# A sixth slot in the ring of norm statistics: every activation tile of a two-layer decoder trunk moves 128 bytes up

## The chip, the cores and the metric

One core of one Trainium2 chip runs the whole program. The metric is device time in microseconds (us). Three runs of the kernel before took 859.58, 862.08 and 862.19 us, so the median is 862.08 us. Lower is better.

## What is computed

The reference is a decoder trunk of two layers on 256 tokens of width 1024, in float32. In each layer:

- h = RMSNorm(x). One projection of h gives the inputs of three token mixers and three gates. The mixers are sliding-window attention, a diagonal state-space recurrence (S5) with a gated linear unit, and a causal convolution of 31 taps with a layer norm.
- The three results, each times the sigmoid of its gate, are added, projected, and added to x.
- A SwiGLU feed-forward of hidden width 2816 follows: x + (silu(RMSNorm(x) Wg) * (RMSNorm(x) Wu)) Wo.
- A gated per-layer embedding is added: x + sigmoid(RMSNorm(x) Wp) * (p We).

A last RMSNorm gives the output. There are thus seven norms: three in each layer and the last one.

## The kernel before

**Tiles and stages.** The 256 tokens are two tiles (t = 0, 1) of 128 partitions. Every product with a weight is done by `gemm` (lines 468 to 488): the weights stream through SBUF in blocks of 128 x 1024 floats (512 KB), each split into a rounded part `wh` (ScalarE, a cast, line 176) and its remainder `wl` (VectorE, a subtraction, line 200). The activations are split the same way into `hi` and `lo` tiles. Each product is three TensorE matmuls of 512 columns, hi*wh, hi*wl and lo*wh, in which the activation slice of 128 x 128 is the loaded (stationary) operand and the weight slice of 128 x 512 is the streamed (moving) one. They are all recorded at line 227, so the rows tell them apart by their tiles: `zk`, `zq`, `zc` and `g` (input projection and gates), `ya`, `yg`, `yc` (mixer outputs), `mo` (mixer projection), `fz` and `fo` (feed-forward in and out), `ez`, `pz` and `pl` (embedding and its gate). `yx` is the S5 output, made of many float32 matmuls of 64 columns. TensorE also does the transposes (line 307: `hT`, `sT` and others).

**Order.** The program is written out in one fixed order for each engine by a planner in the file itself, which books estimated costs per tile and lets small streams of vector and scalar work in between the matmuls. The planner looks at names of tiles and of ring slots that it has given itself (`keys`, line 102), for the weights and the PSUM banks; it does not look at addresses, and the tiles of norm statistics are not among those that it aliases. All DMAs are issued by SP's queue.

**Pools and addresses.** SBUF tiles come from three pools that are laid one after the other in each partition: `cp` (constants, x, the S5 tables), `wp` (the weight rings `raw`, `wh`, `wl`) and `act` (all activation tiles). Inside `act` each tag is a ring of slots, and the rings lie in the order in which their tags are first used. The first call in the schedule is

```python
        def norm_stats():
            return act.tile([128, 16, NT], F32, tag="nst", bufs=5, name="nst")
```

so the ring `nst` is the first of the pool. One tile of it is 16 x 2 floats, 128 bytes per partition. It is asked for seven times, once for each norm: for the first input norm (in the main body), and in each call of `layer` for the feed-forward norm (`fst`), the embedding gate's norm (`pst`) and the next input norm or the last norm (`nst`). With five slots the sixth request (`pst` of the second layer) takes the slot of the first one, and the seventh (the last norm) takes that of the second.

Who touches such a tile: `norm_half` (line 496) sums squares into it on ScalarE (tile `sqj` holds the squares), `norm_end` (line 501) makes 1/sqrt(mean) in it on GpSimd (POOL), and the scalings of `zk`, `zq`, `zc`, `g`, `fz` and `pz` read it.

The byte addresses in each partition, as the built program has them (ring starts; the last column is the address modulo 256, which is the same for all slots of a ring whose slot size is a multiple of 256):

| tiles | pool | start | modulo 256 |
|---|---|---|---|
| x0, x1 | cp | 18112, 22208 | 192 |
| ones, sdT, brow (bias rows and their factors) | cp | 28544, 29056, 30080 | 128 |
| ubuf (convolution input; 1144 bytes per channel half) | cp | 34176 | 128 |
| CAr (S5 table; the matmul for index j reads from byte 640*j + 128 of it) | cp | 44896 | 96 |
| raw, wh, wl | wp | 67424, 79712, 96096 | 96 |
| nst (5 slots) | act | 112480 | 96, then 224 and 96 in turn |
| 4096-byte tiles: feature tiles h, m, f, p (hi and lo), M, e, fgb | act | 113120 | 224 |
| 1024-byte tiles: fth, sqj, cacc, gtm, tb and others | act | 149984 | 224 |
| zqk, vt, kT | act | 161760 | 224 |
| 2048-byte tiles: hd, gt, sT, aT, cT, qT, v, sw and others | act | 168928 | 224 |
| Sr, Si (last) | act | 224672, ends at 228896 | 160 |

Of the kernel before, what the change touches and what calls it, by code (L numbers as in the profile page):

```python
# [6 lines left out]
F32 = mybir.dt.float32  # L7
# [9 lines left out]
NT = 2  # L17
# [64 lines left out]
def trunk_kernel(tc, wts, par, bmat, cst_d, x_d, pos_d, pt_d, bias_d, fg_d, out_d, dbg=None):  # L82
# [3 lines left out]
    with ctx:  # L86
        cp = ctx.enter_context(tc.tile_pool(name="cp", bufs=1))
        wp = ctx.enter_context(tc.tile_pool(name="wp", bufs=5))
        act = ctx.enter_context(tc.tile_pool(name="act", bufs=2))
# [398 lines left out]
                    pump(slack)  # L488

        def norm_stats():  # L490
            return act.tile([128, 16, NT], F32, tag="nst", bufs=5, name="nst")

        def stat(sts, i, t):
            return sts[:, i, t:t + 1]
# [601 lines left out]
        def layer(l, feat, sts, prep):  # L1096
# [156 lines left out]
            mT.upto(2)  # L1253

            fst = norm_stats()
            fT = []

# [52 lines left out]
            def hid_lhs(t, k):  # L1310
                while len(hid) <= k // 2:
                    push()
                return hid[k // 2][0][:, t, k % 2, :], hid[k // 2][1][:, t, k % 2, :]

            pst = norm_stats()
            gT = []
            for n in range(2):
# [16 lines left out]
            gT[0].upto(2)  # L1334

            nst = norm_stats()
            nT = []

# [311 lines left out]
```

## Time and profile before

| | |
|---|---|
| median of three runs | 862.08 us |
| the profiled execution's own time | 860.29 us |
| its span, first to last instruction | 858.5 us |
| mean granted TensorE clock in it | 0.994 of full speed |
| TensorE (PE) busy | 840.4 us, 98% |
| weight loads of TensorE (PEld) busy | 686.8 us, 80% |
| VectorE (DVE) busy | 580.9 us, 68% |
| ScalarE (ACT) busy | 457.2 us, 53% |
| GpSimd (POOL) busy | 126.8 us, 15% |

How to read the profile: times are us from the span's start unless marked ns. A line "L200 DVE TENSOR_TENSOR wl<-raw,wh" is the group of instructions of line 200 on VectorE that write `wl` from `raw` and `wh`. A matmul's own duration (394 ns) is longer than the step from one to the next (233 ns), since matmuls are pipelined; time is lost or won only in the steps. "idle before" is time in which the engine did nothing, with what it waited for.

### The profile page before, as it was taken

How to read it: one execution, taken by the hardware profiler on the slowest of the kernel's cores; microseconds unless marked ns; L12 is line 12 of the kernel's file. 1: busy time of each engine (PE TensorE's matmuls, PEld its weight loads, DVE VectorE, ACT ScalarE, POOL GpSimd, SP SyncE). 2: the span in 40 equal slices, each digit the busy share in tenths (PEclk: the TensorE clock that was granted, in tenths of full speed). 3: DMA queues.
4: the chain of work that ended last, by engine and by line, in shares of the span. 5: the costliest groups of instructions: out<-in, count | busy, mean ns of one | idle time of the engine just before them, and what ended most of it. 6: DMA issues, size and time to landing. Idle time of an engine off the chain costs nothing.

```text
span 858.5 us, 11139 instructions
## 1 busy us (share of the span) xinstructions
PE 840.4 (98%) x3976; PEld 686.8 (80%) x3976; DVE 580.9 (68%) x865; ACT 457.2 (53%) x745; POOL 126.8 (15%) x325
## 2 busy tenths in 40 slices
PE   8989999899999999999999999999999999999996
PEld 7877788688888888888888878878888888888885
DVE  4688875887667784654577599568766666654555
ACT  5675756345556666543564554544554454444454
POOL 5787001000744200000020000100000000000001
PEclk9999999989999999999999999999999999999999
DMA  7554533436765654666654443655566666666661
GB/s 252 181 178 138 152 120 98 123 99 180 211 173 177 187 177 148 179 182 190 184 152 145 124 123 101 191 174 173 172 185 180 182 177 187 181 179 189 182 185 75
DMA packets 41199, 141.34 MB, mean 165 GB/s; under 512 B 4756, under 2 KB 6404, under 8 KB 41144
## 3 DMA queue, kind: packets, MB, share of 16 engines
q1 hardware_dynamic: 41144, 140.64, 55.2%
q8 instruction: 31, 0.51, 0.2%
q14 instruction: 24, 0.20, 0.1%
HBM read 139.49 MB, written 1.13 MB: 164 GB/s over the span
## 4 chain that ended last, share of the span: by engine, by line
PE 88%; ACT 4%; DVE 3%; DMA 2%; POOL 1%; issue 1%; SPq 0%; POOLq 0%; ACTq 0%; DVEq 0%
PE fz L227 29%; PE g L227 15%; PE fo L227 14%; PE mo L227 5%; PE pz L227 4%; PE yg L227 3%; DMA raw<-in_wts 2%; PE ya L227 2%; PE sc L227 2%; PE pl L227 1%; PE zq L227 1%; PE ez L227 1%; PE zc L227 1%; PE yc L227 1%; PE yx L227 1%; ACT wh L176 1%
## 5 line engine op out<-in xcount | busy, mean ns | idle before, releaser
L200 DVE TENSOR_TENSOR wl<-raw,wh 128x1024 fp32r<-128x1024 f32 (+1 forms) x261 | 316.2, 1215 | 212.5 <-ACT wh L176 212.4
L176 ACT CAST wh<-raw 128x1024 fp32r<-128x1024 f32 (+1 forms) x261 | 271.6, 1043 | 205.2 <-PE fo L227 57.0
L200 POOL TENSOR_TENSOR nst<-nst 128x2 f32<-128x2 f32 (+1 forms) x14 | 2.8, 199 | 538.9 <-ACT sqj L171 538.4
L227 PE MATMUL fz<-wh,f0h 128*128 128x512 f32 x176 | 70.9, 403 | 0.0
L227 PE MATMUL fz<-wh,f1h 128*128 128x512 f32 x176 | 70.4, 400 | 0.0
L227 PE MATMUL fo<-wh,hdh 128*128 128x512 f32 x176 | 69.8, 397 | 0.0
L227 PE MATMUL fz<-wh,f1l 128*128 128x512 f32 x176 | 69.6, 395 | 0.0
L227 PE MATMUL fz<-wh,f0l 128*128 128x512 f32 x176 | 69.5, 395 | 0.0
L227 PE MATMUL fo<-wh,hdl 128*128 128x512 f32 x176 | 69.5, 395 | 0.0
L227 PE MATMUL fo<-wl,hdh 128*128 128x512 f32 x176 | 69.5, 395 | 0.0
L227 PE MATMUL fz<-wl,f1h 128*128 128x512 f32 x176 | 69.5, 395 | 0.0
L227 PE MATMUL fz<-wl,f0h 128*128 128x512 f32 x176 | 69.4, 394 | 0.0
L227 PEld LDWEIGHTS fo<-wh,hdl 128*128 128x128 f32 x176 | 33.1, 188 | 7.9
L227 PEld LDWEIGHTS fz<-wh,f1l 128*128 128x128 f32 x176 | 33.1, 188 | 7.9
L227 PEld LDWEIGHTS fz<-wh,f0l 128*128 128x128 f32 x176 | 33.1, 188 | 7.8
L227 PEld LDWEIGHTS fo<-wh,hdh 128*128 128x128 f32 x176 | 33.1, 188 | 7.7
L227 PE MATMUL g<-wh,h1h 128*128 128x512 f32 x96 | 38.7, 403 | 0.6 <-DVE M L210 0.6
L227 PEld LDWEIGHTS fo<-wl,hdh 128*128 128x128 f32 x176 | 33.1, 188 | 7.6
L227 PEld LDWEIGHTS fz<-wl,f1h 128*128 128x128 f32 x176 | 33.1, 188 | 7.5
L227 PEld LDWEIGHTS fz<-wh,f1h 128*128 128x128 f32 x176 | 33.1, 188 | 7.4
L227 PE MATMUL g<-wh,h0h 128*128 128x512 f32 x96 | 39.0, 406 | 0.0
L227 PEld LDWEIGHTS fz<-wl,f0h 128*128 128x128 f32 x176 | 33.2, 188 | 7.2
(390 smaller groups left out, 1766.6 us busy)
## 6 DMA issues: line engine op xcount, KB each, us to landing
raw<-in_wts SPq DMA_DIRECT2D x258, 512.0 KB
raw<-in_wts SPq DMA_DIRECT2D x4, 256.0 KB
out<-e SPq DMA_DIRECT2D x4, 256.0 KB
x<-in_x SPq DMA_DIRECT2D x4, 128.0 KB
x<-in_x SPq DMA_DIRECT2D x2, 256.0 KB
bm<-in_bmat SPq DMA_DIRECT2D x4, 128.0 KB
pT<-in_pt SPq DMA_DIRECT2D x2, 256.0 KB
fgb<-in_fg SPq DMA_DIRECT2D x1, 512.0 KB
```

The source lines that it names most:

```text
L176: ACT.copy(out=out, in_=in_)
L200: (eng or DVE).tensor_tensor(out=out, in0=a, in1=b, op=op)
L227: PE.matmul(out, lhsT, rhs, start=start, stop=stop)
```

## The change

The ring gets a sixth slot:

```diff
         def norm_stats():
-            return act.tile([128, 16, NT], F32, tag="nst", bufs=5, name="nst")
+            return act.tile([128, 16, NT], F32, tag="nst", bufs=6, name="nst")
```

All that lies behind this ring in the pool `act` starts 128 bytes higher; the pools `cp` and `wp` and the ring's first five slots stay where they are. The sixth request for statistics takes a slot of its own, and the seventh takes the slot of the first request. No computing instruction, no transfer and no place in any engine's order is added or taken away by the edited line.

## Rows read from the trace of the kernel before

**Rows 1.** The page's first part: span, and busy time of each engine.

```profile
span 858.5 us, 11139 instructions
PE 840.4 (98%) x3976; PEld 686.8 (80%) x3976; DVE 580.9 (68%) x865; ACT 457.2 (53%) x745; POOL 126.8 (15%) x325
```

**Rows 2.** The page's fourth part: the chain that ended last, by engine.

```profile
PE 88%; ACT 4%; DVE 3%; DMA 2%; POOL 1%; issue 1%; SPq 0%; POOLq 0%; ACTq 0%; DVEq 0%
```

**Rows 3.** The chain of waits in order of time: start, length, what.

```profile
265.31 11.20 PE fz L227 x48
...
382.37 29.27 PE fo L227 x126
...
762.76 29.39 PE fo L227 x126
```

**Rows 4.** Windows of the span: busy (count) by engine, granted clock, DMA share, GB/s.

```profile
core 0: us, PE busy (x) PEld busy (x) DVE busy (x) ACT busy (x) POOL busy (x), PEclk, DMA share, GB/s
165.00:169.80 4.80, 1.83 (x10) 1.21 (x9) 3.28 (x6) 1.95 (x3) 0.00 (x0) 1.00 0.71 219
169.80:176.70 6.90, 5.94 (x16) 4.43 (x16) 3.41 (x7) 1.92 (x3) 0.00 (x0) 0.51 0.24 63
855.80:858.50 2.70, 0.00 (x0) 0.00 (x0) 0.00 (x0) 0.00 (x0) 0.00 (x0) 0.52 0.46 173
```

**Rows 5.** Groups by shape, TensorE, operands moved (hi tiles) and unmoved (brow, sdT).

```profile
L227 PE MATMUL fo<-wl,hdh 128*128 128x512 f32 x176 | 69.5, 395 | 0.0
L227 PE MATMUL fz<-wl,f1h 128*128 128x512 f32 x176 | 69.5, 395 | 0.0
L227 PE MATMUL g<-wl,h1h 128*128 128x512 f32 x96 | 37.9, 394 | 0.0
L227 PE MATMUL g<-brow,sdT 128*128 128x512 f32 x24 | 9.5, 394 | 0.0
```

**Rows 6.** Instructions of tile yx: duration min/median/max in ns, first and last start.

```profile
L227 PEld LDWEIGHTS yx<-Sr,CAr x32: 192/192/193, 160.0 to 476.1; 128*128 128x128 f32 x32
L227 PE MATMUL yx<-Sr,CAr x32: 275/275/276, 160.1 to 476.1; 128*128 128x64 f32 x32
```

**Rows 7.** Instructions of tiles cacc, M, fth and hdh in the same form.

```profile
L210 DVE SCALAR_TENSOR_TENSOR cacc<-ubuf,cst,cacc x58: 433/479/482, 41.7 to 116.4; 128x256 f32<-128x256 f32 x58
...
L200 DVE TENSOR_TENSOR M<-M,gt x8: 691/692/693, 161.2 to 606.0; 128x512 f32<-128x512 f32 x8
L210 DVE SCALAR_TENSOR_TENSOR M<-gt,ya x8: 680/682/689, 133.5 to 579.3; 128x512 f32<-128x512 f32 x8
...
L200 DVE TENSOR_TENSOR M<-scr,cst x2: 683/684/685, 82.5 to 291.3; 128x512 f32<-128x512 f32 x2
...
L171 ACT ACTIVATE fth<-fz,nst x44: 463/475/476, 225.9 to 759.5; 128x256 f32<-128x256 f32 x44
...
L176 ACT CAST hdh<-hT x22: 585/587/588, 230.5 to 762.8; 128x512 fp32r<-128x512 f32 x22
```

**Rows 8.** Instructions of the second feed-forward's end on ScalarE, in order of time.

```profile
790.92 0.63 ACT L171 ACTIVATE sqj<-x 128x512 bf16<-128x512 f32 x1 [1.89 <-DVE x L200]
```

**Rows 9.** The chain of waits around the S5 output of the first layer.

```profile
165.37 1.47 PE ya L227 x6
166.85 0.02 issue
166.87 0.69 DVE M L210
167.56 0.61 DVE ge L200
168.17 0.02 issue
168.19 0.64 ACT ge L171
168.83 0.02 issue
168.85 0.70 DVE gy L210
169.55 0.02 issue
169.58 0.46 DVE gtm L214
170.03 0.04 issue
170.08 1.13 PE sT L307 x4
171.21 0.02 issue
171.23 0.61 ACT sTh L171
171.83 0.04 issue
171.88 8.94 PE yg L227 x28
```

**Rows 10.** TensorE in order of time after that wait.

```profile
171.88 0.79 PE L227 MATMUL yg<-wh,sTh 128*128 128x512 f32 x1 [0.69 <-ACT sTh L171]
...
175.88 0.63 PE L227 MATMUL yg<-wh,sTl 128*128 128x512 f32 x1
176.31 0.55 PE L227 MATMUL yg<-wh,sTh 128*128 128x512 f32 x1
176.70 0.39 PE L227 MATMUL yg<-wl,sTh 128*128 128x512 f32 x1
```

## The prediction

> **What bounds the kernel now.** I read the page's busy times first: TensorE is busy 840.4 of 858.5 us, VectorE 580.9 and ScalarE 457.2 [rows 1]. Then the chain that ended last: 88% of it is TensorE, and all other engines and transfers together are 12% [rows 2]. Then the chain in order of time, to see what TensorE does there: long unbroken runs of 512-column matmuls. In the feed-forward 48 of them take 11.20 us and 126 take 29.27 to 29.39 us, which is 233 ns from one to the next in both [rows 3]. So the time is, nearly everywhere, the number of matmuls times one step. What is not that step is short: the largest hole is 166.85 to 171.88 in the first layer, where the S5 output goes through VectorE and ScalarE before TensorE can take it up [rows 9], and a tail after the last matmul. An edit counts here if it changes the number of matmuls, the length of their step, one of these few holes, or the clock.
>
> The number doesn't change: the edited line adds and takes away no instruction. What is left is where the operands lie and which slot two of the statistics tiles get.
>
> **The slot.** Before, the sixth request for statistics must wait until the first tile has been read for the last time; its first writer is the square-sum that starts at 790.92, and what that instruction in fact waited for is VectorE's update of x [rows 8]. The old tile's readers are the scalings of the first layer's input projection and gates, and in the program's order all of these stand ahead of that layer's `yg` matmuls, which start at 171.88 [rows 9]. The seventh request behaves the same way with the second tile, whose readers end with the first layer's feed-forward, ahead of the `fo` run that starts at 382.37 [rows 3]. With six slots the sixth request waits for nothing and the seventh for the first tile. All these waits are satisfied hundreds of us before they are asked for, so removing or replacing them is worth 0. If a stand-alone wait instruction comes or goes with them, its price is not shown as a row of its own; the nearest rows are the gaps called "issue" in the chain, 0.02 to 0.04 us [rows 9]. Bounds: -0.08 to +0.08 us for two. I take 0.
>
> **The addresses, TensorE.** The moved operands are the stationary slices (`h`, `f`, `hd` and so on) of most 512-column matmuls; the weights stay. Before, the moved tiles lie at 224 modulo 256, after it at 96. No row shows the same tile in both places, so the cost must be bounded by operands that already lie differently. First, the bias matmul `g<-brow,sdT`: both of its operands are in the pool that stays, at 128 modulo 256, and its duration is 394 ns, against 394 and 395 ns for `g<-wl,h1h`, `fz<-wl,f1h` and `fo<-wl,hdh`, whose stationary operand is at 224 and whose moving one is at 96 [rows 5]. Second, and closest to the edit, the S5 output: the matmul for index j reads its table `CAr` from byte 640*j + 128, and 640 is two and a half times 256, so each next j stands exactly 128 bytes further modulo 256. Over 32 such matmuls the loads take 192 to 193 ns and the matmuls 275 to 276 ns [rows 6]. If a shift by 128 bytes mattered to TensorE, these would fall into two groups. So I take 0 per matmul. The bound is one step of the rows' own difference, 1 ns in 395: 0.25%. The three families whose rows stand there have 6 x 176 (`fz`), 3 x 176 (`fo`) and 6 x 96 (`g`) matmuls, 2160 in all, and 2160 x 233 ns = 503 us; 0.25% of that is 1.3 us either way.
>
> **The addresses, VectorE and ScalarE.** The convolution reads `ubuf` from a start that moves by 4 bytes with each of the 29 taps of its long row and by 1144 bytes between the two channel halves, so modulo 256 its 58 instructions sample starts from 132 up to 364, in steps of 4 bytes. Their median is 479 ns and their longest 482, so half of them lie within 3 ns wherever they start [rows 7]. VectorE's 512-element operations run in 680 to 693 ns whether their inputs are both moved tiles (`M<-M,gt`), PSUM and a moved tile (`M<-gt,ya`) or unmoved constants (`M<-scr,cst`) [rows 7]. ScalarE's forms that write moved tiles are as tight over all slots of their rings: 585 to 588 ns and 463 to 476 ns [rows 7]. I take 0. As a bound I use the whole spread of VectorE's rows, 680 against 693, 2%. It would count only where these engines are on the chain: in the hole of [rows 9] they hold 0.69 + 0.61 + 0.64 + 0.70 + 0.46 + 0.61 = 3.71 us, and 2% of it is 0.07 us; all of their share of the chain, 7% of 858.5 or 60 us [rows 2], would give 1.2 us at the very most. Elsewhere the cover is TensorE's own work: VectorE has 32% of the span free [rows 1]. If that cover were gone, a matmul group would start late by what VectorE lost, some 14 ns per operation.
>
> **The addresses, transfers.** The weight stream writes tiles that don't move. Of the moved tiles the one with a transfer at the end is the output, stored from `e`. After the last matmul the queues are busy for 0.46 of 2.70 us, or 1.2 us [rows 4]. I take 0 for it. [...]
>
> **The sum** is 0. Its bounds add up to 1.3 (TensorE) + 1.2 (VectorE and ScalarE) + 0.1 (waits) = 2.6 us either way. The profiled execution took 860.29 us; the shown runs took 859.58, 862.08 and 862.19, so it stands inside their spread of 2.6 us, and the median is near its upper end. With nothing changed I expect the mean of these four, 861.0 us, rather than the median.
>
> **The rivals.** (a) *TensorE's two reads meet.* After the change the stationary tiles stand at 96 modulo 256, as the weights do, while before they stood 128 bytes apart. If reads at the same place in such a stretch got in each other's way, each of the long runs of matmuls would slow down. As a price I take the 2% of VectorE's forms: 2% of the 503 us is 10 us, giving 871 us; it decides the sign from a step longer by 1.2 ns on (2160 x 1.2 ns = 2.6 us). Against it: `brow` and `sdT` already lie at the same place modulo 256, and their matmul takes the usual 394 ns [rows 5]. (b) *The mirror image*: the present place is the bad one and the step of 233 ns has slack that the move frees; 2% would give 851 us. The same row speaks against it. (c) *The clock.* [...] Between 171.88 and 176.70 the `yg` matmuls make eleven steps of 0.43 or 0.44 us instead of 0.233 [rows 10]: 4.82 us against 2.57, a loss of 2.25 us. [...] Without the fall: 860.29 - 2.25 = 858.0 us; with one more: 862.5, or 864.4 in a run like the highest. That two thirds of the runs lie 2.5 us above the third would fit such a difference. (d) *The tiles don't move*, because something else in the pool takes the 128 bytes up: the time would be that of the forecast.
>
> **How the numbers follow.** Two medians of this kernel less than 0.3%, 2.6 us, apart can't be told from no change. The forecast (and (d), which gives the same time) gets 0.78, since three independent rows have operands 128 bytes or less apart without any second group. (b) gets 0.06, and a median without the clock's fall 0.06: faster 0.12. (a) gets 0.06, and a median raised by a second fall 0.04: slower 0.10. The low end of the range is (c) without its fall, 858.0; the high end is the forecast with the sum's upper bound, 861.0 + 2.6 = 863.6, which lies above all shown runs. It leaves out (a), (b), the second fall in a high run and a little of the forecast, about 0.2 in all.
>
> **What would show it.** If right: `fz` still 11.20 us for 48 and `fo` 29.3 for 126; `yx`, `M`, `hdh` and `fth` within 3 ns of [rows 6, 7]; the hole at 167 of 5.0 us, with or without the low clock. Wrong on TensorE: the step off 233 ns by over 1 ns, in the families with moved stationary operands and not in `g<-brow,sdT`. Wrong on the clock: the same steps but another number of low-clock stretches. Wrong on the slot: a new wait on the statistics tiles near 790 or 835 us.

## The result, and the profile after

The changed kernel takes 847.11 us in the median of four runs (846.29 to 849.21), the kernel before 862.13 us in four (859.58 to 862.33). The ratio is 0.9836 with a 95% interval of 0.9811 to 0.9862: about 14 us or 1.6% faster (by the two medians 15 us). The forecast was no change, 858.0 to 863.6 us; rival (b) had the sign, at a chance of 0.06. The profiled execution took 846.92 us, with a span of 845.1 us against 858.5.

The first part of the page, to read beside [rows 1]:

```profile
span 845.1 us, 11139 instructions
PE 825.9 (98%) x3976; PEld 684.2 (81%) x3976; DVE 581.0 (69%) x865; ACT 458.3 (54%) x745; POOL 130.0 (15%) x325
```

The same 11139 instructions ran, in the same order on each engine. VectorE and ScalarE are busy for as long as before, to 0.1 and 1.1 us, GpSimd for 3.2 us longer. TensorE lost 14.5 us of busy time over the same 3976 matmuls. Where, the chain of waits in order of time tells, to read beside [rows 3] (start, length, what):

```profile
262.95 10.91 PE fz L227 x48
...
348.15 28.59 PE fo L227 x126
377.62 28.59 PE fo L227 x126
...
751.31 28.61 PE fo L227 x126
```

126 matmuls of `fo` take 28.59 us instead of 29.27 to 29.39: one step is 28.59 / 126 = 226.9 ns, where it was 232.3 to 233.3. Every long run is shorter: 48 of `fz` take 10.91 or 10.94 us (227.3 or 227.9 ns each) instead of mostly 11.20. Groups by shape, to read beside [rows 5]:

```profile
L227 PE MATMUL fz<-wl,f1h 128*128 128x512 f32 x176 | 68.5, 389 | 0.0
L227 PE MATMUL fo<-wl,hdh 128*128 128x512 f32 x176 | 68.5, 389 | 0.0
L227 PE MATMUL g<-wl,h1h 128*128 128x512 f32 x96 | 37.4, 390 | 0.0
...
L227 PE MATMUL g<-brow,sdT 128*128 128x512 f32 x24 | 9.4, 393 | 0.0
```

The three families with moved operands fell from 394 or 395 ns to 389 or 390. The bias matmul, whose two operands did not move, is at 393 where it was 394: what was taken for proof that place doesn't matter is now the odd one out.

The gain grows with the number of matmuls done. The second `fo` run of the first layer starts at 377.62 instead of 382.37, 4.75 us earlier, and the first of the second layer (751.31 instead of 762.76) 11.45 us earlier. Over all 512-column matmuls that follow one another within 260 ns the step fell from 232.7 to 227.8 ns in the mean. The program has 3096 such products of weights and activations, so that is worth 3096 x 4.9 ns = 15.2 us; the span is 13.4 us shorter. The first part of the gain is lost again early on: where `yx` begins (160.19 us instead of 160.07), nothing is gained yet. Windows of the span (columns as in [rows 4]), of the kernel after:

```profile
36.00:70.00 34.00, 31.00 (x142) 25.05 (x141) 29.57 (x60) 20.81 (x33) 29.54 (x72) 0.95 0.58 181
...
169.80:176.70 6.90, 5.83 (x19) 4.45 (x20) 3.76 (x7) 1.92 (x3) 0.00 (x0) 0.75 0.28 75
```

and of the kernel before:

```profile
36.00:70.00 34.00, 31.67 (x149) 25.37 (x148) 29.02 (x59) 21.78 (x33) 29.47 (x71) 1.00 0.58 177
```

From 36 to 70 us TensorE did 7 matmuls fewer, at a mean granted clock of 0.95 where it was 1.00: a new stretch of low clock, 0.50 from 65.81 to 69.21 us. The stretch after the S5 output is shorter than before instead: 0.50 from 171.62 to 175.03 us where it was 0.50 from 169.82 to 176.63, so that over the window from 169.80 to 176.70 the mean clock is 0.75 where [rows 4] show 0.51. By an estimate from these clocks the first costs 0.05 x 34 = 1.7 us and the second gives 0.24 x 6.9 = 1.7 us back, so the two cancel and are not the gain.

The instructions of VectorE and ScalarE did not change, as in [rows 7]:

```profile
L200 DVE TENSOR_TENSOR M<-M,gt x8: 691/692/692, 161.5 to 598.1; 128x512 f32<-128x512 f32 x8
...
L171 ACT ACTIVATE fth<-fz,nst x44: 463/476/477, 224.4 to 748.2; 128x256 f32<-128x256 f32 x44
```

### The profile page after: what moved, and what is told of

Same layout as the page of the kernel before. It is cut to its first block, busy times and chain, and to the rows that moved or that the text cites. A ratio compares the mean times of both kernels' runs of the same rounds, so it can differ in the third digit from the quotient of the medians.

```text
span 845.1 us, 11139 instructions
## 1 busy us (share of the span) xinstructions
PE 825.9 (98%) x3976; PEld 684.2 (81%) x3976; DVE 581.0 (69%) x865; ACT 458.3 (54%) x745; POOL 130.0 (15%) x325
## 4 chain that ended last, share of the span: by engine, by line
PE 88%; POOL 4%; ACT 3%; issue 1%; DVE 1%; DMA 1%; SPq 1%; POOLq 0%; ACTq 0%; DVEq 0%
PE fz L227 28%; PE g L227 15%; PE fo L227 14%; PE mo L227 5%; PE pz L227 4%; PE yg L227 3%; PE sc L227 2%; PE ya L227 2%; POOL scr L205 2%; PE pl L227 1%; PE zq L227 1%; PE ez L227 1%; PE yc L227 1%; POOL scr L200 1%; PE yx L227 1%
```

## The experiments

Four theories were set against each other. S: the sixth slot frees a wait. P: the place of the loaded (stationary) operand sets TensorE's step. R: what counts is how the loaded operand lies to the streamed one. W: the writes of other engines into the moved tiles disturb TensorE. All kernels give the step of a matmul, read from long runs in the chain of waits as length by count. One run has one time and one profile unless an interval is given.

**The move without the slot, and the slot without the move.**

```diff
+            act.tile([128, 32], F32, tag="pad", bufs=1, name="pad")
             sts = norm_stats()
```

> The ring keeps its five slots; an unused tile of 128 bytes stands in front of it, so the activation tiles lie where the changed kernel has them and the statistics tiles take turns as in the kernel before. Theory P (the place of the loaded operand sets TensorE's step) and its rivals R (the distance between loaded and streamed operand) and W (VectorE's and ScalarE's writes into the moved tiles disturb TensorE's reads): step of the 512-column matmuls 226.7 ns, 48 of fz in 10.9 us, time 847 us within 2. Theory S (the sixth slot frees a wait): step 233.3 ns, 11.20 us, 862 us.

847.83 us in the median of four, ratio 0.9861 (0.9831 to 0.9890). The other way round:

```diff
-            return act.tile([128, 16, NT], F32, tag="nst", bufs=5, name="nst")
+            return act.tile([128, 12, NT], F32, tag="nst", bufs=6, name="nst")
...
+            act.tile([128, 16], F32, tag="pad", bufs=1, name="pad")
             sts = norm_stats()
```

> Six slots of 96 bytes and an unused tile of 64 bytes: 640 bytes as in the kernel before, so no activation tile moves, but the sixth request has a slot of its own. P, R and W: step 233.3 ns, time 862 us within 2. S: 226.7 ns, 847 us.

859.46 us beside 860.11, the median of the kernel before in that session. The chain of the first kernel:

```profile
348.14 28.59 PE fo L227 x126
```

and of the second:

```profile
351.52 29.39 PE fo L227 x126
```

S falls: the slot does nothing that these runs can tell, the 128 bytes do all of it.

**Part of the tiles moves.**

```diff
+            if l == 0:
+                act.tile([128, 32], F32, tag="pad", bufs=1, name="pad")
             S["Ux"] = Ux = b2([128, 8, 64], name="Ux")
```

> An unused tile of 128 bytes ahead of the ring of 2048-byte tiles alone: hd, sT, aT, cT, pT and gt move, the feature tiles h, m, f and p stay. P and R: fo, ya, yg, yc and ez step at 226.7 ns, while fz, g, mo, pz and the input projection stay at 233.3; about 1000 matmuls x 6.6 ns = 6.6 us less, 855 us within 2. W: no split by the loaded operand; fz steps change as much as fo steps, since both run beside the same writes. S: nothing changes, 862 us.

```profile
739.57 11.20 PE fz L227 x48
...
762.79 28.61 PE fo L227 x126
```

`fo`, whose loaded tiles moved, steps at 227 ns; `fz`, beside the same writes in the same run, at 233. W falls, and the gain goes with the operand that a matmul loads. The time, 858.76 us beside 860.11, is less of a gain than forecast. The families that moved hold 816 such products by the program, not about 1000, worth 4 us at 4.9 ns each. Also, this run has a low-clock stretch early on which the profile before lacks (a mean clock of 0.95 from 36 to 70 us, and 0.991 over the run), and `yx` begins at 162.28, 2.2 us behind it.

**Another distance.**

```diff
+            act.tile([128, 8], F32, tag="pad", bufs=1, name="pad")
             sts = norm_stats()
```

> An unused tile of 32 bytes in front: the loaded slices of 512 bytes start on a multiple of 512 instead of 480 (before) or 96 (after) modulo 512. P: if what costs is how a slice lies across a boundary of 512 or 256 bytes, this place has the least of it, step at most 226.7 ns, time at most 847 us. R (a distance of 128 bytes to the weights modulo 256 is bad, none is good; here it is 160 modulo 256): nearer to the kernel before, 230 to 233 ns, 855 to 862 us. S: 862 us.

862.88 us; the chain:

```profile
353.76 29.41 PE fo L227 x126
```

That is 233.4 ns: slices that start exactly on a multiple of 512 bytes are no better. P in its natural form, a slice crossing a boundary, is refuted here.

**Weights and activations move together, and the weights alone.** Both have the first line; the second kernel has one statistics slot fewer, so that the activation tiles stand where they stood.

```diff
         M4 = cp.tile([128, 8, 64], F32, name="M4")
+        cp.tile([128, 32], F32, name="pad")
...
-            return act.tile([128, 16, NT], F32, tag="nst", bufs=5, name="nst")
+            return act.tile([128, 16, NT], F32, tag="nst", bufs=4, name="nst")
```

> An unused tile of 128 bytes at the end of the constants' pool, ahead of the weight rings: weights and activation tiles both move by 128 bytes, so the loaded slices stand where the changed kernel has them and their distance to the weights is that of the kernel before. Theory P (place of the loaded operand alone): step 226.7 ns, fz 10.9 us for 48, time 847 us within 2. Rival R (distance of loaded and streamed operand): step 233 ns, 862 us.

> The same unused tile ahead of the weight rings, and one slot fewer (four) in the ring of statistics: the weights move by 128 bytes, the activation tiles stand where the kernel before has them. P: step 233 ns, 862 us. R: the distance is that of neither kernel; the weights now stand at the same place modulo 512 as the loaded slices, so a change either way from 233 ns, by over 3 ns, 853 us or 870 us.

The chain when both move, 859.91 us:

```profile
352.02 29.29 PE fo L227 x126
```

and when the weights alone move, 846.67 us:

```profile
347.45 28.61 PE fo L227 x126
```

This closes the square. The loaded slices stand at 480 or 96 modulo 512, the weights at 352 or 480, and the step is 233 where they differ by 128 and 227 where they differ by 256 or by nothing. P falls, R stands: in these runs neither place is good or bad, their agreement modulo 256 is. For the second kernel the forecast of R had named a change without its sign.

**A fan of distances in steps of 32 bytes.**

```diff
-            return act.tile(shape, dt, tag="b4", bufs=9, name=name)
+            n = math.prod(shape[1:])
+            v = act.tile([128, n + 8], dt, tag="b4", bufs=9, name=name)[:, 0:n]
+            axes = "abc"[:len(shape) - 1]
...
```

(The rest gives the flat tile its shape again. The second kernel has 160 bytes more in front.)

> Each slot of the ring of 4096-byte tiles is 32 bytes longer, so its nine slots start at 480, 0, 32, 64 and so on to 224 modulo 512, and the ring of 2048-byte tiles stands at 256. P: the steps of g, fz, mo and pz fall into groups by slot: 233 ns in slots at 480 and 0 (as measured there), 226.7 at 96, and unknown in between, with the change of level at one or two places of the 512; fo has one level, that of 256. Rival W (any traffic in the moved tiles): no groups by slot, one step for all. Time between 847 and 862 us.

> As the run before with 160 bytes more in front: the nine slots start at 128, 160 and so on to 384 modulo 512, the 2048-byte tiles at 416. P: 233 ns at 384, where the unmoved bias factor sdT also lies and costs 233 ns in both kernels; some lower slots at 226.7 ns or another level; fo one level. W: no groups by slot. Time between 847 and 864 us.

860.65 and 861.90 us. I sorted the steps of these two runs by the addresses of the program: some 140 steps in which the slice loaded before, the one loaded next and the stream agree modulo 256 take 229.3 ns in the mean, the more than 5000 steps without any agreement 232.6. `fo` has one distance in each run, 160 and 64 bytes modulo 256, and 29.41 and 29.39 us for 126. Taken by groups of three (hi*wh, hi*wl, lo*wh), no pair of distances that occurs more than ten times is near 227: 230.3 to 233.5 ns. The fan does not have a clean row for each distance, though: hi and lo have the same one only at 32, 64, 128 and 160 bytes (232.3 to 233.4 ns), while 96, 192 and 224 occur in mixed groups alone. The forecast of clean groups by slot did not come out, since hi and lo halves of a matrix are in different slots here and agreeing steps stand among others.

**All on one grid, and the changed kernel again.** Weights, activations and bias rows all stand at 128 modulo 256.

```diff
         M4 = cp.tile([128, 8, 64], F32, name="M4")
+        cp.tile([128, 8], F32, name="pad")
...
-            return act.tile([128, 16, NT], F32, tag="nst", bufs=5, name="nst")
+            return act.tile([128, 16, NT], F32, tag="nst", bufs=6, name="nst")
```

> Six slots as in the change, and 32 bytes more at the end of the constants' pool, so weights, activation tiles and the bias rows with their factors (sdT, ones, brow) all start at 128 modulo 256. Theory R256 (a step is 227 ns when loaded and streamed operand start at the same place modulo 256, else 232 to 234): as the changed kernel, and in addition the steps into and out of the 40 bias matmuls fall from 235 and 230 to 227 ns, 12 ns each, 0.5 us in all: 846.5 us within 2. Rival A (the place itself counts too, 96 was a good one): a step other than 227 ns in all families.

> The changed kernel once more, beside the run before on the same chip: 847 us within 1.5, step 226.7 ns, bias steps 235 and 230 ns.

846.89 us, ratio 0.9844 (0.9822 to 0.9866), against 847.38 us, 0.9856 (0.9830 to 0.9882), for the changed kernel on the same chip. TensorE in order of time around a bias matmul, in the changed kernel:

```profile
530.70 0.40 PE L227 MATMUL g<-wh,h1l 128*128 128x512 f32 x1
530.94 0.39 PE L227 MATMUL g<-brow,sdT 128*128 128x512 f32 x1
531.17 0.39 PE L227 MATMUL g<-wh,h1h 128*128 128x512 f32 x1
```

and with all on one grid:

```profile
530.95 0.39 PE L227 MATMUL g<-wh,h1l 128*128 128x512 f32 x1
531.18 0.39 PE L227 MATMUL g<-brow,sdT 128*128 128x512 f32 x1
531.41 0.39 PE L227 MATMUL g<-wh,h1h 128*128 128x512 f32 x1
```

At the trace's full resolution the two steps are 235 and 230 ns in the first and 227 and 227 in the second; over all bias matmuls of a run 234.9 and 230.3 in the mean against 227.0 and 227.7. So the bias factor, loaded while disagreeing weights stream, costs the step before it and its own, and some 10 ns go with it. The 0.5 us are below what the two medians can tell apart.

**One disagreeing operand in three.** The streamed one:

```diff
+                    if i == 0 and tg == "wh":
+                        wp.tile([128, 32], F32, tag="pad", bufs=1, name="pad")
```

> An unused tile of 128 bytes between the rings wh and wl: the activation tiles lie where the changed kernel has them, wh stays and agrees with them modulo 256, wl does not. R256: of three matmuls the one that streams wl is slow and the two that stream wh are fast, or its neighbours take part of the loss; mean step between 228.8 and 231 ns, time 851 to 857 us, and the next steps differ by streamed tile. Rival L (only the loaded operand's place counts after all): 226.7 ns for all, 847 us.

860.33 us; the chain:

```profile
739.73 11.19 PE fz L227 x48
762.89 29.39 PE fo L227 x126
```

I missed this: with `wl` alone 128 bytes apart, two streams in three agree, and yet the whole loss is there, 231 to 233 ns in every family. L falls with it. The forecast that steps differ by streamed tile did come out: in `fo` they take 234.6 ns in the mean from a `wh` stream to the `wl` stream, 232.8 from there to the next, and 230.7 between the two `wh` streams, which agree with every slice around them and are still 4 ns above 227. The loaded one, with the longer slots of the next experiment, hi not offset and lo 128 bytes off:

```diff
-                self.lo = [b4([128, 4, NT, 128], F32R, name=f"{name}l{i}") for i in range(2)]
+                self.lo = [b4([128, 4, NT, 128], F32R, name=f"{name}l{i}", off=32) for i in range(2)]
```

> The lo half of each feature tile is 128 bytes off, the hi half agrees with the weights; fo's tiles agree. Of three matmuls two load an agreeing slice. If one disagreeing operand in three costs the whole loss (as the run with wl apart showed for the streamed side): fz, g and mo at 232 to 233 ns, fo at 226.9, about 857 us. If a disagreeing slice costs only its own two steps (as the bias factor does, 12 ns each): 226.7 + 12/3 = 230.7 ns, about 854 us.

854.29 us:

```profile
735.38 11.11 PE fz L232 x48
...
758.42 28.62 PE fo L232 x126
```

`fz` steps at 231.5 ns, near the second forecast of 230.7, and the steps show why: in the median 233 ns while the lo slice is being loaded, 234 while it is in use, 227 for the third. Here a disagreeing slice costs its own two steps. Why a disagreeing stream in three costs more stays open.

**Offsets in bytes.** Slots of 4352 bytes, and each feature tile starts a few bytes into its slot.

```diff
-            return act.tile(shape, dt, tag="b4", bufs=9, name=name)
+            n = math.prod(shape[1:])
+            v = act.tile([128, n + 64], dt, tag="b4", bufs=9, name=name)[:, off:off + n]
...
-                self.hi = [b4([128, 4, NT, 128], F32R, name=f"{name}h{i}") for i in range(2)]
+                self.hi = [b4([128, 4, NT, 128], F32R, name=f"{name}h{i}", off=OFFS[name]) for i in range(2)]
```

> Slots of 4352 bytes (17 x 256; the 2048-byte ring has 24 slots, to make room), all rings at the changed kernel's place modulo 256, and each feature tile set off by some bytes: f0 4, h0 8, p0 12, f1 16, p1 20, h1 24, m0 28, m1 none; fo has none. If the agreement must be exact to the byte: fo and mo of the second layer at 226.7 ns, all others at 232 to 234, time about 858 us. If it holds within a line of 16 bytes: f0, h0, p0 fast as well, the others slow, about 852 us. If only steps of 32 matter: all fast, 847 us.

852.09 us. The chain of the first layer's `pz` and the second layer's `mo`, `fz` and `fo` (f1 is 16 bytes off, p0 12, m1 and `fo` none):

```profile
413.95 13.60 PE pz L233 x60
428.43 8.28 PE pz L233 x36
...
615.31 9.55 PE mo L233 x42
627.10 12.25 PE fz L233 x54
639.78 11.20 PE fz L233 x48
...
756.04 28.59 PE fo L233 x126
```

None of the three forecasts fits as it stands; that the time is the 852 us of the second is luck, since f0, 4 bytes off and fast by that forecast, steps at 232 to 233 ns. `pz` is at 226.7 ns in its first stretch and at 230 in its second; `fz` is at 226.9 in its first and at 233.3 in all that follow. What the fast first stretches share is what ran just before them: `ez` and `mo` with agreeing tiles. That alone does not do it: the second layer's `pz` (p1, 20 bytes off) follows an agreeing `ez` too, and 48 of them take 11.19 us, 233.1 ns each. The repetition with other offsets (in floats):

```diff
-OFFS = dict(h0=2, m0=7, f0=1, p0=3, h1=6, m1=0, f1=4, p1=5)
+OFFS = dict(h0=3, m0=19, f0=3, p0=3, h1=11, m1=3, f1=11, p1=19)
```

> As the run with offsets in bytes, with other ones: h0, f0, p0 and m1 12 bytes, h1 and f1 44, m0 and p1 76; fo none. If 12 bytes is a second good place (as p0 showed, 88 steps at 227.7 ns): zk, zq, zc, g, fz, pz of the first layer and mo of the second at 227 to 228 ns. If the good places repeat each 32 bytes: h1 and f1 too, and all else, about 848 us. If p0's row was a matter of its neighbours in time and exact agreement modulo 256 is the one good place: 231 to 233 ns for all but fo, about 857 us.

852.71 us. The chain (f0 and p0 12 bytes off, f1 44, m0 76, m1 12):

```profile
230.58 11.21 PE fz L233 x48
...
253.87 11.05 PE fz L233 x48
...
415.85 13.60 PE pz L233 x60
430.33 8.28 PE pz L233 x36
```

At the same 12 bytes `fz` of the first layer, which follows the disagreeing m0, starts at 233.5 ns and goes on at 230.2, while `pz`, which follows the agreeing `ez`, again starts at 226.7. So 12 bytes is no second good place. By these rows a small offset allows several paces, and what ran before has a part in which one it is; that reading was not tested by itself, and the change from 233.5 to 230.2 within one layer's `fz`, with no operand moved, does not follow from it.

## Why the prediction was wrong, step by step

- **What bounds the kernel: right.** The time is the number of matmuls times one step, and the step is what changed, from 232.7 to 227.8 ns in the mean.
- **The slot at 0: right,** by the run with the slot alone (859.46 us beside 860.11).
- **"The addresses, TensorE. ... So I take 0 per matmul", with a bound of 1.3 us: this step failed.** The step fell by 233.3 - 226.9 = 6.4 ns, 2.7%, over ten times the 0.25% of the bound. Both rows that it rested on were read for the wrong quantity. `g<-brow,sdT` was taken as a pair at one place, but each bias matmul stands alone between others: its factor is loaded while `wh` streams, 32 bytes away, and the next slice is loaded while `brow` streams, 96 bytes away modulo 256. Both disagree before the change, and its two steps were slow like all others, 232.4 ns into it and 232.5 out of it in the mean; equal durations between two slow cases said nothing of a fast one. `yx` did sample the table 128 bytes apart, but only the table: a row of `Sr` has 66 floats, so its slices start at 160 + 8j modulo 256 before and 32 + 8j after, the table's at 224 or 96, and no pair agrees in either kernel. So a second group could not show there. It is also a 64-column float32 matmul with a step of its own: 48 of them take 5.31 us in the chain before and 5.30 after, though a third of them (`Ux` with the table `TJ`) come to one place by the change. Rows of the same shape and the same pairing were missing, and the bound should have been left open there.
- **VectorE, ScalarE: right.** 692 and 476 ns as before, within 1 ns.
- **Transfers at 0:** no run isolates them, so neither this nor another small value is shown.
- **Rival (a) had the geometry and the wrong sign:** it noted that after the change loaded and streamed tiles stand at the same place modulo 256, and took that for the bad case. It is the good one. **Rival (b)** had the sign and, at 851 us, most of the size: it priced the step 2% down, it went down 2.7% in `fo`. Both prices also left matmuls out: they count the 2160 of three families, and 3096 have a moved slice.
- **Rival (c), the clock:** its fall is that of the granted clock to 0.51 in [rows 4]. After the change the stretch is there again in a shorter form, 0.75 over the same window, and a new one appears between 36 and 70 us, 0.95 in the mean. By the estimate above they are 1.7 us each, in opposite directions, and not the 14 us. The low end of the range, 858.0 us, leaves the fall out, and the 862.5 us have one more: no trace shows the kernel before in either form. The lowest of its times is 859.52 us, and its one trace has one such fall between its matmuls.
- **What (c) says of the spread** is borne out in part. Beside two of the experiments the kernel before ran 14 times: the three times above 862 us have a mean granted clock of 0.992, the other eleven, 859.52 to 860.60, one of 0.994 or 0.995. By an estimate from these clocks, 0.0025 of 858 us is 2.1 us. In which stretch those three lost it, no trace shows.

## What to carry to other kernels

Where long runs of matmuls like these (float32r, 512 columns, a load for each) bound a kernel, look at where the loaded and the streamed operand start in the partition, modulo 256, and try both rings on the same place: here the step was 227 ns there and 233 ns at 128 bytes apart, a pad of 128 bytes decided 1.6%, and any edit that changes the size of a small tile ahead of a ring can win or lose it unnoticed. Read the step from long runs of the chain, by family, to see whether it is there to be had. A row is evidence on an address only if shape, pairing and neighbours are those of the matmuls in question.

## What the runs showed of the hardware

In these runs a float32r matmul of 512 columns with its 128 x 128 load steps at 226.7 to 227.9 ns, in runs of 48 to 126, when the loaded slices and the streamed slices all start at the same place modulo 256 bytes. At a distance of 32, 64, 128 or 160 bytes it steps at 232 to 234 ns, and at 230 to 234 where hi and lo slices lie at different multiples of 32. Absolute places modulo 512 made no difference: loaded slices and weights at 480 and 480 take 28.57 to 28.61 us for 126 of `fo`, and at 96 and 352 28.59 to 28.61; at 480 and 352 they take 29.27 to 29.39, and at 96 and 480 29.27 to 29.29. Two other forms show no such effect: the float32 matmuls of 64 columns above (5.31 and 5.30 us for 48), and the float32 transposes `hT`, which step at 108.5 ns before and at 108.5 ns with all on one grid, where identity and tile, too, start at the same place. So the step depended on how the addresses of the loaded and the streamed operand lay to each other, 227 against 233 ns. By what mechanism, no run here shows. Nor is it settled why one disagreeing stream in three costs the whole, nor which paces offsets under 32 bytes allow.
